# Two-layer hybrid backbone: four modulation parts computed in the first layer's feed-forward

## The chip, the cores and the metric

The kernel runs on one core of a Trainium2 chip. The metric is the device time of one execution in microseconds (us). The kernel before was run three times: median 2722.55 us, lowest 2719.62, highest 2728.21. One more execution was recorded by the hardware profiler, and all rows below are from that one.

## The reference

The reference computes two layers of a diffusion backbone on 512 latent tokens (and 256 context tokens) of width 1024. Every sub-layer begins with a modulated norm, whose shift and scale come from a small vector `c` by way of a large matrix `w_ada`. Cut to what matters here:

```python
def modnorm(x, gain, shift, scale):
    return rms(x) * gain * (1.0 + scale) + shift
...
# per layer: six modulation vectors of width 1024 for the latent tokens
# and six for the context tokens, from one product with w_ada
...
h = modnorm(x, gain1, shift1, scale1)   # norm1: token mixers
# RWKV-7 recurrence, latent attention, Fourier mixing, merged by gates
x = x + gate1 * mixers(h)
h = modnorm(x, gain2, shift2, scale2)   # norm2: gated ConvFFN
x = x + gate2 * ffn(h)
```

The modulation of a layer depends on `c` and `c_ctx` alone, so any of it can be computed at any time before its first use. The kernel cuts the 2 x 6 x 1024 values into 24 parts, named (layer, j, half): j is 0 for the shift and 1 for the scale of norm1, 2 its gate, 3 to 5 the same of norm2, and a half is 512 columns.

## The kernel before

The residual stream lies transposed, channels on partitions, 768 tokens (512 latent, 256 context) along the free axis. All large products keep fp32 accuracy by splitting: a weight tile of 128 columns is loaded raw into a buffer `wr` (512 KB, `load_w`, L186), ACT copies it rounded into `wh` (L183), DVE makes the rest `wl` (L184), and PE runs three passes (high by high, low by high, high by low; L220 for dense products). The raw buffers are a ring of three (`WR_BUFS`) in one pool, shared by all weight loads; `wh` and `wl` have two buffers each. All weight loads are issued by SP's queue, in the order in which the scheduler put them. The scheduler of the framework orders each engine's instructions when the program is built.

A layer goes through these stages: projections of the recurrence (`rwkv_project`), the recurrence in twelve steps (`rwkv_scan`, lines 942 to 1214), the other mixers (`rwkv_out`, `fourier`, `mla`), the merge with its output products, and the ConvFFN with 22 columns f, of which each takes two loads of `w_up` (products `mm` from `fH`, `fL`), a three-tap convolution (`conv`, ACT L229 and DVE L231, L232), a gate (ACT L1400, DVE L1401) and a split into `gH` and `gL`. In layer 0 the gates of the three branches are computed as background work for PE: `gate_part` makes one gate column in 24 products of 512 tokens and 24 of 256 (L688), from two loads split like any weight, and ACT copies the result (`gt`, L693).

`ada_part` (L234) computes one modulation part: four loads of `w_ada`, 512 KB each, into the same ring `wr` (L245); eight matmuls of 32 columns (L258, 16 instructions on PE in the trace), two per load; a copy `row` by ACT (L261); four transposes (L265); and small operations on DVE (L268, L269, for a scale L272). With `ahead` the next load is issued before the current one's products.

The class `Background` (L699) mixes the gate items and the parts between other work. In the recurrence each slot (`after`) allows so many us of background (2.0 in the first 12 slots, then 1.0): gates first, and between their steps a step of a part (`aside`, PSUM tag "a", with `ahead`). After the recurrence `mix` puts the parts that are left between the gate items, and the mixers call `run` with 2.5 us a time (`MFILL`); these parts use the tag "w", which has one buffer and is the gates' too, and load without `ahead`. Parts (0, 0, ·) and (0, 1, ·) are done at the start; `ADA` lists the other 20, and layer 0 takes the first twelve (`ADAS[0]`): ten of them are started in the recurrence, and the last two, (1, 1, 0) and (1, 1, 1), come in the mixers. `ADAF` lists parts for the ConvFFN of layer 0: part f is computed after the code of column f, without `ahead`, with tag "w". It is empty before.

Of the kernel before, what the change touches and what calls it, by code (L numbers as in the profile page):

```python
# [56 lines left out]
WA_BUFS = 12  # L57
NP = (4, 6)
ADA = [(l, j, hf) for l in range(2) for j in range(6) for hf in range(2)][4:]
ADAS = (ADA[:12], ADA[12:])  # L60
ADAF = ()
LEFT = (99, 0)
FRONT = (False, True)
TAGF, TAGO = ("r", "r"), ("s", "r")
# [18 lines left out]
def hybrid_backbone_kernel(ctx: ExitStack, tc: tile.TileContext, A, out, dbg=None):  # L83
# [1199 lines left out]
    for l in range(DEPTH):  # L1283
# [8 lines left out]
        with ExitStack():  # L1292
            gp = far(yst, l, f"gt{l}")

            items = [("m", i) for i in (5, 6, 7, 2, 3, 4, 0, 1)] + [("g", x, c) for c in range(8) for x in range(3)]
            bg = Background(l, items, ADAS[l], hH, hL, streams, gp)
            with ExitStack() as e2:
# [91 lines left out]
        with ExitStack() as es:  # L1389
            fp = near(es, l, f"ff{l}", 2)  # L1390
            for gi, (f0, f1) in enumerate(FGROUPS):
                gH, gL = [], []
                for f in range(f0, f1):
# [12 lines left out]
                    gL.append(lo)  # L1406
                    if l == 0 and f < len(ADAF):
                        for _ in ada_part(*ADAF[f], "w"):
                            pass
# [124 lines left out]
```

## Time and profile before

| | |
|---|---|
| median of three runs | 2722.55 us |
| the profiled execution, its own time | 2723.43 us |
| its span, first to last instruction | 2721.6 us |
| PE (TensorE matmul) busy | 2581.3 us, 95% |
| DVE busy | 1467.6 us, 54% |
| ACT busy | 1075.3 us, 40% |
| mean granted clock | 0.98 |

The stages of layer 0 in the profile, from its start: recurrence about 229 to 579 us, mixers to 760.7 (first attention product), attention to about 858, merge and output products to 997, ConvFFN to about 1567. Busy time of PE is the sum over instructions as the profiler models their ends; a row of several instructions gives the elapsed time from the first start to the last end.

### The profile page before, as it was taken

The numbers are of one execution on the slowest core, as the hardware profiler recorded it, in microseconds if no ns is written. First come the engines' busy times: TensorE is split into PE (matmuls) and PEld (weight loads), VectorE is DVE, ScalarE is ACT, GpSimd is POOL, SyncE is SP. The second block draws the span as 40 slices with busy tenths as digits, with TensorE's granted clock in tenths as the row PEclk, the third lists the DMA queues.
The fourth block names the chain that finished last, engine by engine and source line by source line (L and its number), as shares of the span: only waits on it lengthen the run. The fifth ranks groups of instructions, "written<-read, shape, count | busy, mean of one in ns | idle before, by whom it ended". The sixth has DMA issues, their size and how long they took to land.

```text
span 2721.6 us, 56800 instructions
## 1 busy us (share of the span) xinstructions
PE 2581.3 (95%) x24016; PEld 2062.2 (76%) x24016; DVE 1467.6 (54%) x2965; ACT 1075.3 (40%) x1914; POOL 234.5 (9%) x316
## 2 busy tenths in 40 slices
PE   6999999997999989999999999999988899899999
PEld 3876777776877878888888877677666678778778
DVE  5443555434556665444444564446554767645546
ACT  4452343433464343222222445444433664423333
POOL 0122122200010000000000001312220010000000
PEclk9998999998999999999999999999999999999999
DMA  6366455365323532222212244764434326332334
GB/s 260 95 163 196 151 156 163 106 209 166 98 99 101 158 93 60 64 62 60 66 54 70 79 155 114 234 201 144 141 111 154 117 83 207 101 93 84 100 96 124
DMA packets 161267, 339.45 MB, mean 125 GB/s; under 512 B 32083, under 2 KB 76757, under 8 KB 161013
## 3 DMA queue, kind: packets, MB, share of 16 engines
q1 hardware_dynamic: 124852, 273.93, 32.4%
q0 software_dynamic: 10944, 36.58, 5.1%
q10 hardware_dynamic: 25216, 25.30, 2.8%
q8 instruction: 190, 3.11, 0.5%
q14 instruction: 65, 0.52, 0.1%
HBM read 273.88 MB, written 61.87 MB: 123 GB/s over the span
## 4 chain that ended last, share of the span: by engine, by line
PE 86%; DVE 5%; DMA 4%; ACT 3%; issue 2%; SPq 0%; ACTq 0%; DVEq 0%; POOL 0%; POOLq 0%
PE mm L220 47%; PE w L688 15%; PE st L957 3%; PE i L957 3%; PE mm L567 2%; PE a L258 2%; PE r L595 2%; PE mm L394 2%; PE s L584 1%; DMA wr<-in_w_ada 1%; PE s L871 1%; PE f L957 1%; PE i L954 1%; DVE wl L184 1%; PE f L954 1%
## 5 line engine op out<-in xcount | busy, mean ns | idle before, releaser
L183 ACT ACTIVATE wh<-wr 128x1024 fp32r<-128x1024 f32 (+4 forms) x334 | 302.0, 906 | 378.5 <-PE mm L220 282.8
L184 DVE TENSOR_TENSOR wl<-wr,wh 128x1024 fp32r<-128x1024 f32 (+3 forms) x332 | 342.6, 1034 | 89.2 <-ACT wh L183 86.8
L220 PE MATMUL mm<-fH,wh 128*128 128x512 f32 (+1 forms) x1072 | 225.0, 358 | 10.5 <-DVE ab L232 7.4
L231 DVE SCALAR_TENSOR_TENSOR ab<-mm,prm,ab 128x511 f32<-128x511 f32 (+1 forms) x132 | 86.8, 657 | 264.2 <-ACT ab L229 264.2
L220 PE MATMUL mm<-fH,wl 128*128 128x512 f32 (+1 forms) x1072 | 220.5, 353 | 0.0
L220 PE MATMUL mm<-fL,wh 128*128 128x512 f32 (+1 forms) x1072 | 219.3, 352 | 0.0
L220 PEld LDWEIGHTS mm<-fH,wh 128*128 128x128 f32 x1072 | 178.7, 192 | 42.1 <-issue 6.4
L220 PEld LDWEIGHTS mm<-fH,wl 128*128 128x128 f32 x1072 | 176.1, 189 | 29.9
L220 PEld LDWEIGHTS mm<-fL,wh 128*128 128x128 f32 x1072 | 175.0, 188 | 29.4
L688 PE MATMUL w<-hH,wh 128*128 128x512 f32 (+1 forms) x760 | 183.9, 377 | 10.2 <-ACT gt L693 9.7
L220 PE MATMUL mm<-gH,wh 128*128 128x512 f32 (+1 forms) x568 | 174.5, 346 | 10.0 <-ACT wh L183 4.8
L688 PE MATMUL w<-hL,wh 128*128 128x512 f32 (+1 forms) x760 | 180.5, 366 | 0.0
L688 PE MATMUL w<-hH,wl 128*128 128x512 f32 (+1 forms) x760 | 177.1, 366 | 0.0
L220 PE MATMUL mm<-gH,wl 128*128 128x512 f32 (+1 forms) x568 | 175.4, 348 | 1.1 <-DVE wl L184 0.9
L1252 DVE SCALAR_TENSOR_TENSOR x<-mm,mod,x 128x256 f32<-128x256 f32 (+1 forms) x136 | 80.0, 606 | 175.1 <-PE mm L220 174.4
L220 PE MATMUL mm<-gL,wh 128*128 128x512 f32 (+1 forms) x568 | 171.6, 343 | 0.0
L688 PEld LDWEIGHTS w<-hH,wh 128*128 128x128 f32 x760 | 125.3, 192 | 45.2 <-ACT gt L693 15.7
L229 ACT ACTIVATE ab<-mm,prm 128x768 f32<-128x768 f32 (+1 forms) x88 | 70.0, 795 | 219.9 <-PE mm L220 219.9
L688 PEld LDWEIGHTS w<-hH,wl 128*128 128x128 f32 x760 | 127.1, 191 | 23.5 <-issue 2.5
L688 PEld LDWEIGHTS w<-hL,wh 128*128 128x128 f32 x760 | 124.5, 189 | 24.0 <-issue 4.0
L220 PEld LDWEIGHTS mm<-gH,wh 128*128 128x128 f32 x568 | 97.3, 188 | 29.8 <-ACT wh L183 10.4
L220 PEld LDWEIGHTS mm<-gH,wl 128*128 128x128 f32 x568 | 97.3, 188 | 17.5 <-DVE wl L184 3.7
(388 smaller groups left out, 4631.4 us busy)
## 6 DMA issues: line engine op xcount, KB each, us to landing
wr<-in_w_up SPq DMA_DIRECT2D x88, 512.0 KB, 3.5
wr<-in_w_ada SPq DMA_DIRECT2D x80, 512.0 KB, 5.2
wr<-in_w_g SPq DMA_DIRECT2D x48, 512.0 KB, 4.1
wr<-in_w_out SPq DMA_DIRECT2D x32, 512.0 KB, 3.6
wr<-in_w_dn SPq DMA_DIRECT2D x48, 320.0 KB, 3.0
X<-rwx SPq DMA_DIRECT2D x48, 288.0 KB, 4.7
wr<-in_w_rw SPq DMA_DIRECT2D x24, 512.0 KB, 4.2
wr<-in_w_dn SPq DMA_DIRECT2D x32, 384.0 KB, 3.2
```

What stands on the lines that cost most here:

```text
L183: S.activation(out=H, in_=raw, func=AF.Copy)
L184: e.tensor_tensor(out=L, in0=raw, in1=H.bitcast(F32), op=ALU.subtract)
L220: TE.matmul(ps[:, a:b], lhsT=W[:, k, :], rhs=X[k][:, a:b], start=(k == 0 and n == 0), stop=(k == kt - 1 and n == 2))
L229: S.activation(out=o[:, a:b], in_=ps[:, a:b], func=AF.Identity, scale=w[1])
L231: V.scalar_tensor_tensor(out=o[:, a + 1:b], in0=ps[:, a:b - 1], scalar=w[0], in1=o[:, a + 1:b], op0=ALU.mult, op1=ALU.add)
L258: TE.matmul(ps[32 * i:32 * i + 32], lhsT=cs32[:, k, :], rhs=w[:, k - k0], start=(k < 4), stop=(k >= 4))
L394: TE.matmul(ps[:, o:o + hi - lo], lhsT=X(k)[:, t * 128:(t + 1) * 128], rhs=W[:, k, lo:hi], start=(k == 0 and n == 0), stop=(k == kt - 1 an ...
L567: TE.matmul(ps[:, a:b], lhsT=qT[:, h, t * 128:(t + 1) * 128], rhs=kT[:, h, a:b], start=True, stop=True)
L595: TE.matmul(po[64 * p:64 * p + 64, 0:128], lhsT=Vn[:, j, h * 64:(h + 1) * 64], rhs=pts[p][:, j * 128:(j + 1) * 128], start=(j == kts[0]), ...
L688: TE.matmul(ps, lhsT=w[:, k, :], rhs=X[k][:, a:b], start=(k == 0 and n == 0), stop=(k == 7 and n == 2))
L957: self.i = f(*a, **k)
L1252: V.scalar_tensor_tensor(out=x[:, a:b], in0=ps[:, a:b], scalar=mod[l][:, j, c, s:s + 1], in1=x[:, a:b], op0=ALU.mult, op1=ALU.add)
```

## The change

Eight parts stay beside the recurrence and the mixers of layer 0, and the four parts of layer 1's norm1, shift and scale, two halves each, are listed for the ConvFFN. The loop there is in the kernel before too.

```diff
-ADAS = (ADA[:12], ADA[12:])
-ADAF = ()
+ADAS = (ADA[:8], ADA[12:])
+ADAF = ADA[8:12]
```

The list sets what the scheduler gets, and so the order on the engines. In the mixers, PE's rows around the end of part (1, 1, 1) in the kernel before are these; L1233, L801 and L813 are the head norms of `rwkv_out`, L657 to L660 the Fourier products, and `w_8100` is the part's PSUM tile.

```order
L813 MATMUL s_7678<-cst_75,rex_7676 128x128 x4
L813 MATMUL s_7683<-cst_75,rex_7676 128x128 x2
L258 MATMUL w_8100<-wr_8101,cs32_102 32x512 x2
L1233 MATMUL s_7718<-y_7709,cst_75 128x512
L657 MATMUL r_7955<-dft_7795,z_7818 128x129
L658 MATMUL r_7955<-alt_7798,zh_7819 128x129
L660 MATMUL r_7955<-dft_7795,z_7818 128x127
L1233 MATMUL s_7721<-y_7709,cst_75 128x256
L258 MATMUL w_8100<-wr_8105,cs32_102 32x512 x2
L258 MATMUL w_8100<-wr_8127,cs32_102 32x512 x2
L801 MATMUL s_7725<-cst_75,y1_7710 128x2 x6
L258 MATMUL w_8100<-wr_8131,cs32_102 32x512 x2
```

After the change the same steps of `rwkv_out` (its `s` tiles have other numbers) stand among gate products.

```order
L813 MATMUL s_7626<-cst_75,rex_7624 128x128 x4
L813 MATMUL s_7631<-cst_75,rex_7624 128x128 x2
L688 MATMUL w_8186<-hL2_151,wh_7880 128x256
L688 MATMUL w_8186<-hL3_152,wh_7880 128x256
L688 MATMUL w_8186<-hL4_153,wh_7880 128x256
L688 MATMUL w_8186<-hL5_154,wh_7880 128x256
L688 MATMUL w_8186<-hL6_155,wh_7880 128x256
L688 MATMUL w_8186<-hL7_156,wh_7880 128x256
L657 MATMUL r_7906<-dft_7743,z_7766 128x129
L658 MATMUL r_7906<-alt_7746,zh_7767 128x129
L660 MATMUL r_7906<-dft_7743,z_7766 128x127
L1233 MATMUL s_7666<-y_7657,cst_75 128x512
```

The products L258 are gone from the place, and L688 follow each other there (16 of 512 tokens behind the last row shown, before the next L1233).

At the end of the mixers PE transposes the query heads (L452, one group of six for each of six token tiles), and the attention's first product is L567. Before, gates stand between them; these rows are followed by 22 wide gate products and the last group:

```order
L688 MATMUL w_8974<-hL5_154,wh_8778 128x256
L688 MATMUL w_8974<-hL6_155,wh_8778 128x256
L452 MATMUL mm_8908<-cst_75,qn_8563 96x128 x6
L688 MATMUL w_8974<-hL7_156,wh_8778 128x256
L452 MATMUL mm_8943<-cst_75,qn_8563 96x128 x6
L452 MATMUL mm_8966<-cst_75,qn_8563 96x128 x6
```

Of the kernel after the change, from the last gate products to the attention's first:

```order
L688 MATMUL w_8932<-hL6_155,wh_8784 128x256
L688 MATMUL w_8932<-hL7_156,wh_8784 128x256
L452 MATMUL mm_8771<-cst_75,qn_8503 96x128 x6
L452 MATMUL mm_8808<-cst_75,qn_8503 96x128 x6
L452 MATMUL mm_8834<-cst_75,qn_8503 96x128 x6
L452 MATMUL mm_8872<-cst_75,qn_8503 96x128 x6
L452 MATMUL mm_8899<-cst_75,qn_8503 96x128 x6
L452 MATMUL mm_8921<-cst_75,qn_8503 96x128 x6
L567 MATMUL mm_8985<-kT_7928,qT_7927 128x512
L567 MATMUL mm_8985<-kT_7928,qT_7927 128x256
```

No gate product is left behind the first L452; before, 24 half-wide and 22 wide ones stand between the second group of transposes and the last, and 2 wide and 24 half-wide ones within the attention.

In the ConvFFN, PE's rows at the border of columns 2 and 3, before:

```order
L220 MATMUL mm_11690<-fL6_10725,wh_11684 128x512
L220 MATMUL mm_11690<-fL6_10725,wh_11684 128x256
L220 MATMUL mm_11690<-fL7_10726,wh_11684 128x512
L220 MATMUL mm_11690<-fL7_10726,wh_11684 128x256
L220 MATMUL mm_11817<-fH0_10711,wh_11806 128x512
L220 MATMUL mm_11817<-fH0_10711,wh_11806 128x256
```

and after, with part (1, 1, 0) in `w_11751`:

```order
L220 MATMUL mm_11636<-fL6_10619,wh_11630 128x256
L220 MATMUL mm_11636<-fL7_10620,wh_11630 128x512
L220 MATMUL mm_11636<-fL7_10620,wh_11630 128x256
L258 MATMUL w_11751<-wr_11752,cs32_102 32x512 x2
L258 MATMUL w_11751<-wr_11756,cs32_102 32x512 x2
L258 MATMUL w_11751<-wr_11760,cs32_102 32x512 x2
L258 MATMUL w_11751<-wr_11764,cs32_102 32x512 x2
L265 MATMUL w_11770<-cst_75,row_11768 128x128 x4
L220 MATMUL mm_11790<-fH0_10605,wh_11779 128x512
```

The part's eight products and four transposes stand between the last product of column 2 and the first of column 3. The same is so for part (1, 1, 1) at the border of columns 3 and 4; of part (1, 0, 1) seven eighths at the border of columns 0 and 1, and of part (1, 0, 0) the first load's products stand ahead of column 0 and the others before its context half (rows 4267 to 4271). SP's queue has these loads in this order, with the semaphores each waits for:

```order
L245 DMA wr_11752<-in_w_ada 128x1024 [waits DMAHW6_49,DVE_49]
L245 DMA wr_11756<-in_w_ada 128x1024 [waits DMAHW5_49,PE_49]
L245 DMA wr_11760<-in_w_ada 128x1024 [waits DMAHW7_49,DVE_49]
L245 DMA wr_11764<-in_w_ada 128x1024 [waits DMAHW0_49,PE_49]
L191 DMA wr_11778<-in_w_up 128x1024 [waits DMAHW1_49,PE_49]
L191 DMA wr_11784<-in_w_up 128x1024 [waits DMAHW2_49,PE_49]
L245 DMA wr_11907<-in_w_ada 128x1024 [waits DMAHW3_49,PE_49]
```

Before, the loads of `w_up` follow each other and each waits for DVE (`wl` of the load three places back). Now a load waits for DVE where that buffer held a `w_up` tile and for PE where it held a part's: `wr_11764`, the fourth of part (1, 1, 0), for the products of its first, `wr_11778` and `wr_11784` (column 3) for those of its second and third.

## Rows read from the trace of the kernel before

**Rows 1.** The page, part 4: the chain that ended last, by line.

```profile
PE mm L220 47%; PE w L688 15%; PE st L957 3%; PE i L957 3%; PE mm L567 2%; PE a L258 2%; PE r L595 2%; PE mm L394 2%; PE s L584 1%; DMA wr<-in_w_ada 1%; PE s L871 1%; PE f L957 1%; PE i L954 1%; DVE wl L184 1%; PE f L954 1%
```

**Rows 2.** Windows: us from and to, length, busy of each engine (count), PEclk, DMA share, GB/s.

```profile
579.00:760.70 181.70, 161.34 (x933) 135.69 (x934) 84.86 (x225) 70.55 (x117) 2.30 (x5) 0.92 0.47 154
...
630.00:640.00 10.00, 4.57 (x16) 2.82 (x16) 1.88 (x13) 0.00 (x0) 0.00 (x0) 0.50 0.92 305
...
1022.00:1567.00 545.00, 539.33 (x3033) 467.00 (x3034) 258.63 (x374) 156.13 (x189) 0.00 (x0) 0.99 0.22 66
```

**Rows 3.** Waits of PE, 579 to 761: total us, times, longest.

```profile
PE w L258 <- DMA wr<-in_w_ada: 10.7, 4, 5.4
PE w L688 <- ACT gt L693: 3.9, 3, 2.8
```

**Rows 4.** Timeline of PE, mixers: start, us, instruction, count, idle before and its releaser.

```profile
610.98 1.40 PE L801 MATMUL s<-cst,y 128*128 128x2 f32 x12
...
626.75 1.05 PE L258 MATMUL w<-wr,cs 128*32 128x512 f32 x4 [1.56 <-DMA wr<-in_w_ada]
...
635.09 2.72 PE L801 MATMUL s<-cst,y 128*128 128x2 f32 x12
641.35 1.92 PE L258 MATMUL w<-wr,cs 128*32 128x512 f32 x4 [3.54 <-DMA wr<-in_w_ada]
...
646.01 3.36 PE L688 MATMUL w<-hH,wh 128*128 128x512 f32 x8
...
732.92 2.02 PE L688 MATMUL w<-hH,wh 128*128 128x512 f32 x8
```

**Rows 5.** Products L258 in the recurrence: its group (229 to 580), then one timeline row.

```profile
L258 PE MATMUL a<-wr,cs 128*32 128x512 f32 x148 | 34.4, 604 | 0.1
...
559.37 1.91 PE L258 MATMUL a<-wr,cs 128*32 128x512 f32 x12
```

**Rows 6.** Lines of PE, 579 to 760.7: count, busy us, mean ns, idle before.

```profile
L258 PE MATMUL w<-wr,cs 128*32 128x512 f32 x32 | 9.3, 718 | 10.7 <-DMA wr<-in_w_ada 10.7
...
L265 PE MATMUL w<-cst,row 128*128 128x128 f32 x8 | 1.7, 354 | 0.7 <-ACT row L261 0.7
```

**Rows 7.** Timeline of ACT and of DVE at the query heads.

```profile
733.12 0.74 ACT L505 ACTIVATE jq<-mm,yc 128x576 f32<-128x576 f32 x1
...
749.31 1.69 ACT L453 ACTIVATE qT<-mm,gT 96x768 f32<-96x768 f32 x2
...
744.92 0.62 DVE L446 TENSOR_TENSOR qn<-qn,sw 128x192 f32<-128x192 f32 x2
```

**Rows 8.** Issues of w_up on SP, then landing times of all loads of line 245.

```profile
993.86 4.50 SPq L191 DMA_DIRECT2D wr<-in_w_up  x2
...
DMA to landing us min/median/max: 3.9/5.3/10.2
```

**Rows 9.** Timeline of PE, columns 0 and 1 of the first feed-forward.

```profile
997.03 2.11 PE L220 MATMUL mm<-fH,wh 128*128 128x512 f32 x8 [0.98 <-DVE x L1252]
...
1010.58 3.19 PE L220 MATMUL mm<-fH,wh 128*128 128x256 f32 x15 [1.05 <-ACT fH L332]
...
1016.00 1.72 PE L220 MATMUL mm<-fL,wh 128*128 128x256 f32 x13
1022.82 5.24 PE L220 MATMUL mm<-fH,wh 128*128 128x512 f32 x16 [5.11 <-DVE ab L232]
...
1027.90 2.97 PE L220 MATMUL mm<-fH,wl 128*128 128x512 f32 x16
```

**Rows 10.** Timeline of ACT: a part's row (mixers), wh and gH (columns 0, 1).

```profile
643.32 0.60 ACT L261 ACTIVATE row<-w 128x512 f32<-128x512 f32 x1 [13.59 <-PE w L258]
...
1020.16 1.05 ACT L183 ACTIVATE wh<-wr 128x1024 fp32r<-128x1024 f32 x1
...
1026.47 0.84 ACT L183 ACTIVATE gH<-ab 128x768 fp32r<-128x768 f32 x1 [1.58 <-DVE ab L1401]
```


## The prediction

> **What bounds the kernel now.** I read the chain of waits first, by line: nearly all of it is products on PE, and of the other entries one is a transfer, 1% of the span, for the modulation weights [rows 1]. So PE sets the time, and a change counts by the PE work and the PE idle time that it moves. Next the stages by windows [rows 2]: the feed-forward of layer 0 has PE busy 539.3 of 545 us at a DMA share of 0.22; the mixers, from the last recurrence step to the first attention product, have it busy 161.3 of 181.7 at 0.47. In the mixers' worst stretch, 630 to 640, PE is busy 4.6 of 10 us, the DMA share is 0.92 and the granted clock 0.50, the lower of its two levels (1.2 against 2.4 GHz). The table of waits tells who ends PE's idle time there: the weight loads of `ada_part` (10.7 us in 4 waits), then ACT's copies of gate results (3.9) [rows 3]. The timeline shows the price: a wait of 3.5 us before one load's products, which then take 1.92 us instead of 1.05, and the next work slow too: the head sums at L801 take 2.72 us against 1.40, eight gate products 3.36 against 2.02 [rows 4]. The reader should see that parts 10 and 11 in the mixers are served late, and that the feed-forward has free DMA time but hardly any free PE time.
>
> **Recurrence: two parts leave.** `a` products took 34.4 us for 148, so 16 of them (one part) 3.7 us of busy time; elapsed, 12 took 1.91, so 2.5 a part [rows 5]. Four transposes cost 0.85 (1.7 us for 8) [rows 6]. The slots are filled all the same: by the order, 19 more 512-wide gate products go ahead of the last state, at 0.25 us each (2.02 for 8, [rows 4]) 4.8 us. The gain is 2 x (2.5 + 0.85) - 4.8 = 1.9, or 4.3 with 3.7 a part. I take 2.5, nearer the elapsed figure. The parts' loads leave SP's queue too; the rows give them no wait worth a term.
>
> **Mixers: two parts leave.** From 161.3 us of PE work go 9.3 and 1.7 [rows 6], the slow clock's excess of 1.3 and 1.3 (above), and the gates' difference: 17 wide products fewer (4.2), 24 half-wide more (3.2), for the gates that stood in the attention are now ahead of it. That leaves 146.7. Of 20.4 us idle the 10.7 go, 9.7 stay. New idle comes at the query heads. Now PE covers them with gates: from the last query product (ACT's read of it at 733.12) to the first rotated tile (744.92 and 0.3) are 12 us [rows 7], and PE was busy. After the change the gates have run out: behind the last query product stand nine half-wide gate products (1.2 us) and then all transposes of the heads. The DVE chain is shorter by 0.7 for a narrower weight split, so PE idles 11.4 - 1.2 = 10.2 us, and 1 more because the six groups of transposes follow ACT's copies at 0.85 each (1.69 for two). The stretch is 146.7 + 9.7 + 11.2 = 167.6, 14.1 less than now, and the attention is rid of 2 wide and 24 half-wide products, 3.6. I take a gain of **18**, with scan **20.5**. Bounds: 33 if other work covers the heads; 10 if the waits of `rwkv_out`'s chain, now hidden behind late loads, come to light.
>
> **Feed-forward: four parts arrive.** Their sixteen loads go through the same three buffers as the weights of the columns. In SP's order each column's two loads stand behind the four loads of the part before, and a buffer is free when PE has used it, so a load is issued late and PE then waits for its landing. Nothing in this stage shows such a landing; the `in_w_ada` loads took 3.9 us at least, 5.3 in the median [rows 8]. I take 3.9, as the stage's DMA share is low [rows 2], and keep 5.3 for the range. By the Trainium skill, DMA: Bandwidth & Descriptors, section Anatomy of one DMA, a transfer takes about 2.0 us and its bytes at 436 GB/s; an estimate from it is 3.2 us for 512 KB, and with that the sum would be about 3.5 us lower, over five landings. No row of a 512 KB load of these weights is so short, so the sum stays with 3.9.
> - Part 0 (behind column 0 in the program): its first products stand ahead of column 0's on PE. Column 0 began at 997.03 [rows 9]; the load takes the third place, issued at 993.86 [rows 8], lands at 997.8, and its products take 1.05 [rows 4]: 1.8 us late. Three more loads' products, at 0.64 (a third of 1.91), stand before the context half: 1.9. The transposes (0.85) fit into the 1.05 us that PE waits for `fH` there [rows 9]. Sum 3.7.
> - Part 1: column 0 ended at t0 = 1017.7 and column 1 began 5.1 us later [rows 9]. Now loads 1 and 2 are each issued after the products of the load before: t0 + 3.9 + 1.05 + 3.9 + 1.05 = t0 + 9.9, 4.8 later. Loads 0 and 3 (0.64 each) and the transposes add 2.1. Sum 6.9.
> - Parts 2 and 3: today column follows column without a gap. Now load 3 is issued after load 0's products, and ACT, in order, must copy the row before it makes `gH` and the next column's `wh`, which the column's products need: 0.64 + 3.9 + 1.05 + 0.60 (row) + 0.84 (gH) + 1.05 (wh) = 8.1 us [rows 10], then a start at the low clock, as at 1022.82 after 5.1 us of idling, where sixteen products took 5.24 against 2.97 [rows 9]: 2.3. Sum 10.4 each.
>
> The losses are 3.7 + 6.9 + 20.8 = **31.4** (27 without the clock's fall, 38 at landings of 5.3). DVE's and ACT's small operations of a part hide beside PE as before, other than those named. Net -20.5 + 31.4 = +10.9 on the profiled execution's 2723.4, which lies 0.9 above the median of 2722.55. **Forecast: 2733.5 us**, slower; its own range is 2724 to 2746.
>
> **Rivals.**
> - Hidden loads, not slower: the stage with a DMA share of 0.22 takes sixteen loads without PE seeing them; paid is PE work alone, 4 x (2.5 + 0.85) = 13.4. Then -20.5 + 13.4 gives 2716 (2706 at the gain's upper bound). It decides at the third buffer: if a load is issued a landing (3.9 us) before PE comes to it. Low DMA share speaks for it, the order of buffer releases against: load 3 waits for load 0's products right ahead of it. This is also what the Trainium skill, Perfetto Trace Analysis, section Optimization Strategy, would have one expect: stages with different most-contended engines gain when interleaved. The rows agree that the engines differ [rows 2].
> - Cancelling: the heads' wait is covered, so the gain is about 31 and the losses equal it: 2723. For it: gates may slide less than I read. Against it: the order shows no gate row left there.
> - The mixers give little: with the late loads gone, `rwkv_out`'s own chain (transfers, DVE, PE by turns) ends the waits, the gain is about 8: 2723.4 - 8 + 31.4 = 2747. For it: the chain's steps lie among the late loads [rows 4]; against: PE has gates to fill with until the heads.
>
> **How the numbers follow.** Forecast 0.51, hidden loads 0.15, cancelling 0.20, little gain 0.14. The range 2712 to 2750 leaves out the lower part of the first rival and the ends of the last. A measurement of this kernel can tell about 0.3% (8.2 us) from no change, so bounds are 2714.4 and 2730.7. Faster: about half of the hidden loads and a little of the rest, 0.11. Slower: two thirds of the forecast's case and nearly all of the last, 0.48. Same: 0.41.
>
> **What would show it.** After the change PE's waits for `in_w_ada` are gone between the recurrence and the attention, and appear in layer 0's feed-forward: one around 8 to 11 us in all ahead of each of columns 3 and 4, two landings in a row ahead of column 1. PE idles some 10 us before the heads' transposes. If the columns follow without gaps, the hidden loads are right and I am wrong; if the stretch to the attention stays near 180 us, the last rival is.

## The result, and the profile after

The changed kernel took 2742.05 us (median of 5 runs, 2740.06 to 2750.11) against 2720.45 (2718.54 to 2728.21) of the kernel before on the same chip: ratio 1.0078, 95% interval [1.0054, 1.0103]. The forecast was 2733.5, slower; the measured time lies within the range, and the loss is about double the one forecast. The profiled execution has a span of 2738.3 us, 16.7 more than before.

Both sides of the prediction stand in the new profile. First the waits of PE (total us, times, longest), from the end of the recurrence to the attention:

```profile
PE mm L452 <- DVE qn L446: 10.1, 1, 10.1
PE w L688 <- ACT gt L693: 8.9, 4, 4.1
```

and from 970 to 1200 us, the end of the output products and the first half of the feed-forward's columns:

```profile
PE w L258 <- DMA wr<-in_w_ada: 16.3, 5, 4.2
PE mm L220 <- DVE wl L184: 3.7, 3, 2.3
PE w L265 <- ACT row L261: 2.1, 3, 0.7
```

The loads' waits [rows 3] are gone from the mixers and have come to the feed-forward, 16.3 us where 10.7 were, ahead of columns 0, 1, 3 and 4. The wait at the query heads, 10.1 us, is new, and the waits for ACT's gate copies have grown from 3.9 to 8.9. The stretch from the recurrence to the attention, by windows (from and to, length, busy of PE, PEld, DVE, ACT, POOL, granted clock, DMA share, GB/s; answers to the first of [rows 2]), and the 5 us around the start of column 3:

```profile
571.00:743.50 172.50, 151.17 (x898) 132.87 (x897) 84.76 (x218) 70.69 (x119) 6.55 (x13) 0.93 0.47 160
```

```profile
1060.00:1065.00 5.00, 3.87 (x13) 3.09 (x14) 3.25 (x6) 3.13 (x4) 0.00 (x0) 0.50 0.42 129
```

The border of columns 2 and 3, as the chain that ended last sees it (start, us, what):

```profile
1053.36 1.02 PE w L258 x8
1054.38 4.32 DMA wr<-in_w_ada
1058.70 0.04 issue
1058.74 1.15 PE w L258 x4
1059.89 0.02 issue
1059.91 0.60 ACT row L261
1060.51 0.73 ACT gH L183
1061.25 0.95 ACT wh L183
1062.20 0.04 issue
1062.24 3.99 PE mm L220 x11
```

Three loads' products follow column 2 at once (1.91 us from 1053.29). The fourth load is issued at 1054.38, when the first load's products have freed its buffer, and lands 4.32 us later, and then products, ACT's row, `gH` and `wh` follow one another until column 3 can begin at 1062.24, 8.9 us late and at a clock of 0.50. At the border of columns 0 and 1 two landings follow each other, as forecast:

```profile
1005.17 3.99 DMA wr<-in_w_ada
...
1009.20 1.95 PE w L258 x4
...
1011.16 4.14 DMA wr<-in_w_ada
...
1015.35 1.92 PE w L258 x4
```

PE's timeline has the rest: the heads, part 0's last three loads and transposes, and column 3, which answers to column 1 in [rows 9].

```profile
736.20 7.17 PE L452 MATMUL mm<-cst,qn 128*96 128x128 f32 x36 [10.10 <-DVE qn L446]
743.54 1.99 PE L567 MATMUL mm<-kT,qT 96*128 96x512 f32 x5 [0.16 <-ACT qT L453]
```

```profile
992.95 1.91 PE L258 MATMUL w<-wr,cs 128*32 128x512 f32 x12
...
996.19 0.66 PE L265 MATMUL w<-cst,row 128*128 128x128 f32 x4 [0.69 <-ACT row L261]
...
1062.24 6.00 PE L220 MATMUL mm<-fH,wh 128*128 128x512 f32 x22 [0.56 <-ACT wh L183]
1068.08 2.96 PE L220 MATMUL mm<-fH,wl 128*128 128x512 f32 x16
```

The 36 transposes of the heads took 7.17 us after the idle time, and the first 22 products of column 3 took 6.00, where 16 take 2.96 a little later.

### The profile page after: what moved, and what is told of

The parts are those of the page before. It is cut to its first block, busy times and chain, and to the rows that moved or that the text cites. A ratio compares the mean times of both kernels' runs of the same rounds, so it can differ in the third digit from the quotient of the medians.

```text
span 2738.3 us, 56818 instructions
## 1 busy us (share of the span) xinstructions
PE 2585.5 (94%) x24016; PEld 2059.2 (75%) x24016; DVE 1469.3 (54%) x2965; ACT 1074.9 (39%) x1914; POOL 233.4 (9%) x316
## 4 chain that ended last, share of the span: by engine, by line
PE 86%; DVE 5%; DMA 4%; ACT 3%; issue 2%; SPq 0%; ACTq 0%; DVEq 0%; POOL 0%; POOLq 0%
PE mm L220 47%; PE w L688 15%; PE i L957 3%; PE mm L567 3%; PE st L957 3%; PE a L258 2%; PE r L595 2%; PE mm L394 2%; PE s L584 1%; DMA wr<-in_w_ada 1%; PE s L871 1%; DVE wl L184 1%; PE f L957 1%; PE i L954 1%; DMA raw<-m_dram 1%
## 5 line engine op out<-in xcount | busy, mean ns | idle before, releaser
L220 PE MATMUL mm<-fH,wh 128*128 128x512 f32 (+1 forms) x1072 | 226.4, 360 | 3.9 <-DVE ab L232 1.7
L220 PE MATMUL mm<-fH,wl 128*128 128x512 f32 (+1 forms) x1072 | 219.9, 352 | 0.0
L220 PE MATMUL mm<-fL,wh 128*128 128x512 f32 (+1 forms) x1072 | 219.9, 352 | 0.0
L220 PEld LDWEIGHTS mm<-fH,wh 128*128 128x128 f32 x1072 | 179.7, 193 | 39.2 <-issue 2.5
L220 PEld LDWEIGHTS mm<-fL,wh 128*128 128x128 f32 x1072 | 175.2, 188 | 31.2 <-issue 1.7
L220 PEld LDWEIGHTS mm<-fH,wl 128*128 128x128 f32 x1072 | 175.3, 188 | 29.5
L688 PE MATMUL w<-hH,wh 128*128 128x512 f32 (+1 forms) x760 | 184.2, 378 | 13.2 <-ACT gt L693 13.0
L220 PE MATMUL mm<-gH,wh 128*128 128x512 f32 (+1 forms) x568 | 175.3, 348 | 10.0 <-ACT wh L183 4.4
L688 PE MATMUL w<-hL,wh 128*128 128x512 f32 (+1 forms) x760 | 182.6, 368 | 0.0
L688 PE MATMUL w<-hH,wl 128*128 128x512 f32 (+1 forms) x760 | 178.6, 367 | 0.2 <-issue 0.2
L220 PE MATMUL mm<-gH,wl 128*128 128x512 f32 (+1 forms) x568 | 175.7, 348 | 1.2 <-DVE wl L184 1.0
L220 PE MATMUL mm<-gL,wh 128*128 128x512 f32 (+1 forms) x568 | 172.4, 345 | 0.0
L688 PEld LDWEIGHTS w<-hH,wh 128*128 128x128 f32 x760 | 124.9, 192 | 47.6 <-ACT gt L693 19.4
L688 PEld LDWEIGHTS w<-hH,wl 128*128 128x128 f32 x760 | 127.8, 193 | 23.2 <-issue 2.2
L688 PEld LDWEIGHTS w<-hL,wh 128*128 128x128 f32 x760 | 125.2, 190 | 23.0 <-issue 3.0
L220 PEld LDWEIGHTS mm<-gH,wh 128*128 128x128 f32 x568 | 97.8, 189 | 29.7 <-ACT wh L183 10.4
L220 PEld LDWEIGHTS mm<-gH,wl 128*128 128x128 f32 x568 | 98.0, 189 | 17.9 <-DVE wl L184 4.1
```

The source lines that it names most:

```text
L220: TE.matmul(ps[:, a:b], lhsT=W[:, k, :], rhs=X[k][:, a:b], start=(k == 0 and n == 0), stop=(k == kt - 1 and n == 2))
L688: TE.matmul(ps, lhsT=w[:, k, :], rhs=X[k][:, a:b], start=(k == 0 and n == 0), stop=(k == 7 and n == 2))
```

## Experiments

Each kernel was compared with the kernel before on the same chip (medians of 2725.5 to 2727 there). The table gives the ratio with its interval, and from the profile of each the start of four products, in us from the start of its execution: the recurrence's last (L957), the attention's first (L567), the attention's last output (L595), the last of the feed-forward of layer 0 (L220 on `gH`). The last column is the way from the third to the fourth, that is, what the feed-forward and the merge before it took.

| kernel | ratio | recurrence | attention | its end | feed-forward | between |
|---|---|---|---|---|---|---|
| before | 1 | 578.7 | 760.7 | 856.0 | 1573.4 | 717.4 |
| changed | 1.0078 [1.0054, 1.0103] | 570.8 | 743.5 | 836.9 | 1591.5 | 754.6 |
| e1_own | 0.9993 [0.9977, 1.0009] | 573.5 | 747.2 | 840.5 | 1567.0 | 726.5 |
| e2_two | 0.9983 [0.9970, 0.9997] | 576.6 | 741.6 | 834.9 | 1564.6 | 729.7 |
| e3_spread | 1.0035 [1.0021, 1.0048] | 572.3 | 744.3 | 837.7 | 1579.9 | 742.2 |
| e4_none | 0.9940 [0.9922, 0.9957] | 574.7 | 749.0 | 842.3 | 1562.8 | 720.5 |
| e5_two_own | 0.9946 [0.9928, 0.9964] | 574.4 | 740.5 | 833.9 | 1552.9 | 719.0 |
| e6_two_gap | 0.9965 [0.9947, 0.9984] | 577.0 | 742.2 | 835.5 | 1557.3 | 721.8 |
| e7_mix_ahead | 0.9994 [0.9977, 1.0011] | 575.7 | 758.8 | 854.1 | 1571.9 | 717.8 |
| e8_hold | 0.9925 [0.9897, 0.9952] | 560.5 | 728.5 | 821.9 | 1549.1 | 727.2 |
| e9_ring_hold | 1.0014 [1.0003, 1.0026] | 559.2 | 726.2 | 819.5 | 1575.0 | 755.5 |
| e10_before_hold | 0.9961 [0.9948, 0.9974] | 561.0 | 742.4 | 846.0 | 1562.8 | 716.8 |
| e11_hold3 | 0.9980 [0.9965, 0.9995] | 571.0 | 748.0 | 841.4 | 1569.2 | 727.8 |
| e12_two_hold | 0.9888 [0.9866, 0.9911] | 560.4 | 730.9 | 826.2 | 1546.2 | 720.0 |

Single executions scatter: the changed kernel, e1_own, e3_spread and e4_none have one and the same order on PE up to the output products, and their attention ends between 836.9 and 842.3. Differences of 5 us between two profiles tell nothing. In layer 1, behind the table, the scatter is larger: from its last product to the end the profiles take 1145.8 to 1159.6 us (1148.2 before, 1157.0 in e5_two_own, 1159.6 in e8_hold). So the ratio tells what a kernel is worth, and the table only where time goes.

**e1_own: buffers of their own.**

```diff
-                        for _ in ada_part(*ADAF[f], "w"):
+                        for _ in ada_part(*ADAF[f], "w", wf, bufs=4):
```

(`wf` is a pool on the feed-forward's side that is closed behind column 3; its tiles are `wa` in place of `wr`.)

> The four parts stay behind columns 0 to 3, but their loads have four buffers of their own and no longer share the ring of three with the feed-forward's weights. Theory (late loads: a ring buffer is free only when PE has used it, so PE waits for landings and restarts at the low clock): the 36 us that the feed-forward gave back fall to the products and transposes, four times 2.6 to 3.4 = 10 to 14, so 2711 to 2716 us, and the waits for in_w_ada (16.3 us) are gone. Rival (the work itself costs it: products, transposes, ACT's copy of the row ahead of gH and wh): still 2735 or more.

The ratio falls from 1.0078 to 0.9993, some 23 us, and the way from the attention's end to the feed-forward's from 754.6 to 726.5. PE waits for no load of a part any more; these are its longest waits from 965 to 1570:

```profile
PE mm L220 <- DVE ab L232: 4.7, 2, 3.3
PE mm L220 <- DVE wl L184: 4.1, 5, 2.3
```

So the loss was the shared ring, not the work: 9 us remain against 37. (With their own buffers the scheduler also put most of part 0's products into the wait for column 0's convolution, so the 9 us are not four whole parts. A longer ring, still shared, was not tried.) On the time itself the theory had 4.5 to 9.5 us below the kernel before (2720.5 when it was written); 2724.31 against 2725.54 is 1.2, as the other side gave less than 19 (e4_none): the theory held in the waits and missed in the time. The rival, 15 above, is out.

**e4_none: the gain by itself.**

```diff
-ADAF = ADA[8:12]
+ADAF = ()
+    P.memset(mod[1][:, 0:2], 0.0)
+    P.memset(gsc[1][:, 0], 1.0)
```

> The four parts are left out altogether (layer 1's first norm uses constants in place of its shift and scale), so this shows the gain of taking them from the recurrence and the mixers by itself. Theory: 19 us, as the attention's end moved, so 2700 to 2703. Rival (the attention's end is an illusion and part of it is given back further on in the layer, so the feed-forward costs less than 36): 2706 or more.

The kernel leaves the four parts out, and layer 1's first norm uses constants. 2710.53 against 2725.54: 15 us, with an interval of 12 to 21. The rival's bound was 14.5 us (2706 against 2720.5), the theory's 17.5 to 20.5, so the interval takes in both, and the middle stands at the rival's edge. In its profile the attention ends 13.7 us earlier than before. So taking the four parts away is worth about 15 us, and with the changed kernel's 21.6 (interval 15 to 28) the feed-forward's cost comes to 36.6, near the table's last column (37.2).

**e2_two: the mixers' parts alone.**

```diff
-ADAS = (ADA[:8], ADA[12:])
-ADAF = ADA[8:12]
+ADAS = (ADA[:10], ADA[12:])
+ADAF = ADA[10:12]
```

> Only the mixers' two parts move (behind columns 0 and 1); the recurrence keeps its ten. Theory: the mixers' gain comes whole (11 to 14 us to the attention's end), the feed-forward gives back 6.1 + 5.2 for the parts at columns 0 and 1: 2717 to 2721, no difference that can be told. Rival (the gain comes mostly from the recurrence, whose end moved by 7.9 us in the changed kernel): gain 5 at most, 2726 or more.

2722.07 against 2725.54, 3.5 us less: the theory's bounds were 3.5 below to 0.5 above the kernel before, the rival's 5.5 above or more, so the rival is out. Two parts moved bring the attention's end forward by 21.1 us, where 11 to 14 were expected, and no less than four. The waits from 570 to 760 tell why:

```profile
PE w L688 <- ACT gt L693: 5.8, 5, 3.4
...
PE mm L452 <- ACT qT L453: 0.8, 2, 0.6
```

No wait of 10.1 us at the heads: with the recurrence's parts in place 19 wide gate products fewer are done in it, and 24 half-wide ones still stand between the heads' transposes. So, as far as single profiles tell, moving the recurrence's two parts took nothing off the path to the attention's end; what the recurrence lost (its end, 570.8 against 576.6) came back as the wait at the heads.

**e3_spread: one load per column.**

```diff
-                    if l == 0 and f < len(ADAF):
-                        for _ in ada_part(*ADAF[f], "w"):
-                            pass
+                    if l == 0:
+                        ada_step(f)
```

(`ada_step` takes the part's generator one load further, and at the fifth column does row, transposes and sums.)

> The same four parts, the same ring, but one load with its two products per column instead of four loads at one column (row, transposes and sums at the fifth): each load has a whole column to land. Theory (late loads): no wait is left, the feed-forward pays the work alone, 10 to 14 us, so 2711 to 2716. Rival (sharing the ring by itself, or the work, costs): 2730 or more.

The waits went, as the theory had it (1.9 us are left), but the time is 2735.73 against 2725.54, 1.0035, at the rival's bound of 9.5 us above. Of the rival's two reasons it was the work. The lines of PE show it, in e1_own and then here (count, busy us, mean ns, idle before):

```profile
L258 PE MATMUL w<-wa,cs 128*32 128x512 f32 x64 | 9.6, 628 | 0.0
```

```profile
L258 PE MATMUL w<-wr,cs 128*32 128x512 f32 x64 | 16.8, 605 | 1.9 <-DMA wr<-in_w_ada 1.9
```

The same 64 instructions took 9.6 us mostly in groups of 16 and 16.8 in groups of four, though each lasts as long (628 and 605 ns). On the timelines a group of four between two columns takes 1.05 us, one of sixteen 1.92:

```profile
1066.91 1.05 PE L258 MATMUL w<-wr,cs 128*32 128x512 f32 x4
```

```profile
1018.91 1.92 PE L258 MATMUL w<-wa,cs 128*32 128x512 f32 x16
```

In the traces, four of the sixteen start within 0.03 us, and the next four about 0.45 us after them; in a group of four, two start and then two. So one load's products alone leave half of what can run side by side unused, and twelve take as long as sixteen (1.91, part 0 above).

Column follows column at 18.0 us here and at 16.8 without a part; a whole part at one border costs 2.5 (19.3 in e1_own). Sixteen groups at 1.2, the transposes of four parts and 1.9 of waits make 24 of the 25 us of the table. So the shared ring costs little if each load has time, but small groups of these products are dear. Small groups with buffers of their own were not tried.

**e5_two_own and e6_two_gap: two parts, own buffers.** e5_two_own is e1_own with the lists of e2_two; e6_two_gap puts both parts behind column 0:

```diff
+                    if l == 0 and f == 0:
+                        for a in ADAF:
+                            for _ in ada_part(*a, "s", wf, bufs=8):
+                                pass
```

> Only the mixers' two parts move (behind columns 0 and 1), and their loads have four buffers of their own. Theory (late loads, and gates that still cover the query heads since the recurrence keeps its parts): the mixers' gain of e2_two stays (21 us to the attention's end by its trace), the feed-forward gives back about 5 (2.5 a part) in place of 12: 7 us below e2_two, 0.994 of the kernel before, and no wait of PE for the loads in either place. Rival (the four parts' order was the matter and the ring is not): as e2_two, 0.998.

> As e5_two_own, but both parts behind column 0, with eight buffers, so that their products stand in the 5.1 us for which PE waits for the convolution there anyway. Theory: nearly nothing is given back (0 to 3 us), 0.992 to 0.994 of the kernel before. Rival (the products delay the next column's start by their own length, since its conv is what is late and the work of ACT and DVE for the parts comes on top): 0.995 or more.

e5_two_own came out as expected: 0.9946, and 719.0 us on the way where the kernel without the parts had 720.5. Part 0's products lie in the wait for column 0's convolution, which shrinks to 2.57 us from 5.11, and column 1 starts at the full pace, with 3.08 us for 16 products and not 5.24 [rows 9]; part 1 costs 2.5.

```profile
1001.45 3.08 PE L220 MATMUL mm<-fH,wh 128*128 128x512 f32 x16 [2.57 <-DVE ab L232]
```

e6_two_gap, 0.9965, does not gain on it. Its second part did not fall into the gap but in four groups into column 1's products, at 1.05 us each, and between the first part's groups PE waited for landings (0.74 and less). Its rival expected 0.995 or more, but for another reason, the lateness of the convolution, and the profile does not show that.

**e7_mix_ahead: ask earlier, move nothing.**

```diff
-                return ada_part(it[1], it[2], it[3], "w")
+                return ada_part(it[1], it[2], it[3], "w", ahead=True)
```

> The kernel before with nothing moved; the two parts in the mixers ask for each load one step ahead. Theory (loads late because the ring's buffers are freed late and the DMA queues are full there): the program's order of issue changes little, so half of the 10.7 us of waits goes at most; 0.998 to 1.000. Rival (the loads are late only because the code asks for them late): the waits go, 11 to 17 us, 0.994 to 0.996.

0.9994, no change, and the wait is what it was [rows 3]:

```profile
PE w L258 <- DMA wr<-in_w_ada: 10.6, 4, 5.0
```

But the edit did not make the loads earlier: SP's queue issues its 789 transfers in the same order in both kernels. So the run decides nothing between the theory and the rival. It shows only that the place of the request in the code does not set the issue here. SP's own waits in the kernel before, from 580 to 640 us, say what held these loads:

```profile
SPq L245 <- PE w L258: 7.4, 4, 3.8
SPq L245 <- DMA wr<-in_w_ada: 3.9, 2, 2.1
```

The larger share is a wait for a part's own products to free a buffer. How much the full queues add was not told apart.

**e8_hold to e12_two_hold: gates held back.** All have 7 or 3 in place of 12 slots of 2.0 us:

```diff
-FIRST = ((12, 2.0), (8, 3.0))
+FIRST = ((7, 2.0), (8, 3.0))
```

e8_hold is e1_own with it, e9_ring_hold the changed kernel, e10_before_hold the kernel before, e12_two_hold is e5_two_own; e11_hold3 is e1_own with 3.

> As e1_own (four parts moved, own buffers), but 7 in place of 12 slots of the recurrence allow 2.0 us of background, so that gates are held back for the mixers. Theory (with the recurrence's two parts gone, gates are used up early and nothing covers the query heads, 10 us): PE's wait of 10.1 us at the heads shrinks to 2 at most, the gates' work leaves the recurrence, so 4 to 8 us below e1_own, about 0.997 of the kernel before. Rival (the wait there is hidden or is taken up by the attention): as e1_own, 0.999.

> The changed kernel (shared ring, four loads at a column) with the gates held back as in e8_hold (7 slots of 2.0 us in place of 12). Theory (two separate losses: the ring in the feed-forward, and the uncovered query heads): the feed-forward still gives back some 36 us, the heads' wait of 10.1 us is gone, so it lies as far below the changed kernel (1.0078) as e8_hold below e1_own (0.007): 1.000 to 1.002. Rival (e8_hold's gain needs the parts' own buffers, since the ring is what the held gates' loads wait for): 1.005 or more.

> The kernel before with the same 7 slots and nothing moved. Theory: its query heads are covered and its gates only go from the recurrence to the attention, so it stays as it is: 0.998 to 1.001. Rival (a shorter background in the first slots is a gain by itself, whatever is moved): 0.995 or less.

> As e8_hold, with 3 slots of 2.0 us. Theory: the heads are covered already at 7 (wait 1.1 us), so holding more gates back gives nothing more: 0.991 to 0.994, as e8_hold. Rival (the gain of e8_hold is the recurrence's shorter slots, which go on paying): 0.990 or less.

> As e5_two_own (the mixers' two parts alone, own buffers), with 7 slots of 2.0 us. Theory: there the gates cover the heads without it, so nothing is gained on e5_two_own: 0.993 to 0.996. Rival (the shorter slots are a gain by themselves): 0.990 or less.

In e8_hold the wait at the heads is nearly gone:

```profile
721.39 1.10 PE L688 MATMUL w<-hL,wh 128*128 128x256 f32 x8
722.33 1.47 PE L452 MATMUL mm<-cst,qn 128*96 128x128 f32 x12
724.87 1.49 PE L452 MATMUL mm<-cst,qn 128*96 128x128 f32 x12 [1.07 <-DVE qn L446]
```

The last gate products now end as the first tiles are ready. But e8_hold gained 0.0068 on e1_own, some 18 us where 4 to 8 were expected, and e10_before_hold and e12_two_hold gained where the theory gave them nothing: 0.0039 and 0.0058. So holding back is a gain by itself, as the rivals had it (e12_two_hold reached its rival's bound of 0.990, e10_before_hold at 0.9961 neither 0.998 nor 0.995), and the theory was too narrow. The attention's end seems to separate the two effects: where the heads were covered before, it moved by 10.0 (before to e10) and 7.7 (e5 to e12); where they were not, by 18.6 (e1 to e8) and 17.4 (changed to e9). The difference, 7 to 11 us, is about the 9 by which the wait at the heads shrank. The runs' own times do not show that split: they gained 10 and 16 us where the heads were covered and 18 and 17 where not, each uncertain by 4 to 9 us, so its size rests on single profiles. The first effect lies in the recurrence. Its end came 17.7 us earlier in e10_before_hold, for 24 wide and 24 half-wide gate products fewer (9.1 us at 0.25 and 0.13); part of the rest is less idling of PE in it. From 300 to 400, of the kernel before, of e10_before_hold and of e11_hold3:

```profile
300.00:400.00 100.00, 95.77 (x2184) 74.39 (x2182) 54.99 (x137) 39.52 (x103) 21.73 (x28) 1.00 0.46 141
```

```profile
300.00:400.00 100.00, 98.66 (x2247) 74.69 (x2235) 57.49 (x144) 39.86 (x106) 25.18 (x32) 1.00 0.51 149
```

```profile
300.00:400.00 100.00, 95.37 (x2089) 70.94 (x2086) 51.34 (x129) 39.23 (x100) 24.64 (x31) 1.00 0.53 160
```

PE is busy 98.7 of 100 us with 7 slots, and 95.8 and 95.4 with 12 and 3 (e11_hold3 is built on e1_own, where it is 96.2 with 12 and 99.6 with 7). At 3, moreover, PE waits 15.2 us for gate copies in the mixers, and e11_hold3, 0.9980, met neither expectation. So of the three numbers tried 7 is best; that it is a matter of where the gates fall between the recurrence's steps is likely, but the cause stays open. e9_ring_hold met its expectation, 1.0014: the feed-forward still took 755.5.

**The version that beats both** is e12_two_hold, 2695.75 us against 2726.97, 0.9888 [0.9866, 0.9911]: the mixers' two parts in the feed-forward with buffers of their own, the recurrence's parts where they were, and fewer gates in the first slots.

## Why the prediction was right, and where it was off

- The sign held, and so did the mechanism of the loss: late loads in the feed-forward. Rival "hidden loads" failed at the third buffer, where the prediction said it would be decided; with own buffers (e1_own) its case becomes true, and what is left is the work.
- By the Trainium skill (Perfetto Trace Analysis, Optimization Strategy) performance may be improved by interleaving stages with different most-contended engines. The rows do not show that these two stages differ so, as the prediction read them: PE is the busiest engine in both (161.3 of 181.7 us and 539.3 of 545 [rows 2]), and the DMA share of 0.92 belongs to 10 us. The runs fall on both sides: the change 1.0078, e5_two_own 0.9946. What decided was the moved loads' buffers.
- Borders of columns 2 and 3, and 3 and 4: forecast 8.1 and 2.3 for the clock, 10.4 each; measured 8.9 and 2.1, 11.0, at the first (column ends at 1053.3 and 1081.1, 27.8 apart, where 16.8 is the pace), and 9.4 and 1.5 at the second. The landing was 4.32, not 3.9.
- Parts 0 and 1: forecast 3.7 + 6.9 = 10.6, measured 13.7 (column 2's end lies 5.4 us ahead of the kernel before, the attention's end 19.1). The two serial landings took 3.99 and 4.14, and the products behind them 1.92 each, at a granted clock of 0.50, where the prediction had 1.05: that is 1.7 of the 3. Part 0's other products ahead of the context half took 1.91, as forecast, and PE waited 0.69 for its row besides.
- The landing: the estimate from the Trainium skill (DMA: Bandwidth & Descriptors, Anatomy of one DMA) was 3.2 us, the row's lower bound 3.9; the chain shows 3.99, 4.14 and 4.32. The row decides, and it was itself a little low. (The page gives its fit for transfers issued by GpSimd; these are issued by SP.)
- Sum of the feed-forward: 31.4 forecast, 37.2 by profile, 36.6 by the runs (1.5 us of it at a later column, in other kernels too).
- The heads: idle time 10.2 forecast, 10.1 measured. Behind it PE was busy 7.17 us with the 36 transposes, where the kernel before has 4.74; the prediction had allowed 1 us for ACT's pace.
- The gain: 20.5 forecast to the attention's end; 13.7 to 19.1 in the four profiles of the same order, 15 by e4_none's time, with an interval of 12 to 21 that takes in the forecast. Between recurrence and attention PE was to be busy 146.7 and idle 20.9 of 167.6 us; it is busy 151.2 and idle 21.3 of 172.5. So the idle time came out in sum, but not in its parts: the waits for gate copies grew from 3.9 us to 8.9, and the other waits that were to stay (for `Vn` 2.5, and shorter ones) shrank. With the parts gone, gates follow gates through the one buffer of tag "w", and PE waits for ACT's copy more often; that this is the reason is read from the order and was not tried.
- **The step that failed** is the price of the low clock behind the new waits. The prediction priced it in one place, 2.3 us at each of columns 3 and 4. "That leaves 146.7" takes the old waits' slow work out of the mixers and puts none in for the new waits, and the products behind the two landings in a row are counted at 1.05 us. The changed kernel shows the clock at its lower level, 0.50, in these places too (windows as above):

```profile
578.30:585.10 6.80, 5.82 (x25) 5.62 (x26) 0.96 (x1) 0.90 (x3) 0.00 (x0) 0.50 1.01 377
736.20:742.10 5.90, 5.90 (x28) 5.28 (x29) 1.87 (x9) 3.22 (x4) 0.00 (x0) 0.50 0.00 1
1009.20:1011.20 2.00, 1.92 (x4) 0.19 (x4) 2.00 (x4) 0.46 (x2) 0.00 (x0) 0.50 0.00 0
```

The first is behind a wait for a gate copy. There eight half-wide gate products take 2.07 us, where eight took 1.22 just before:

```profile
570.95 1.22 PE L688 MATMUL w<-hH,wh 128*128 128x256 f32 x8
...
579.28 2.07 PE L688 MATMUL w<-hH,wh 128*128 128x256 f32 x8 [4.06 <-ACT gt L693]
```

The second is the heads' transposes, the third the products at the border of columns 0 and 1. In the mixers the clock stands at 0.50 for 23.8 us, with PE busy in 15.0 of them; before, with the late loads, it was 27.3 and 17.9. So the low clock moved with the waits instead of leaving. The transposes' excess is 2.4 us, and that of the half-wide gates at 0.50, 39 against 15 before, by estimate as much (at 0.13 us each at full speed). Together that is about the 4.5 us by which PE was busy longer in the mixers than forecast; smaller terms of either sign stand beside it. In the feed-forward it is 1.7 of the 5.8 us of extra cost (37.2 for 31.4); longer landings, the wait for the row and the later column make most of the others. In this profile the recurrence's end, 5.4 us earlier than forecast, happened to make up for the mixers' 4.9, so that its gain (19.1) looks nearer to the forecast than its terms were. By the runs, 5.5 us of the 10.7 between the loss and its forecast (21.6 and 10.9) lie on the side of the gain (15 for 20.5) and 5.2 in the feed-forward, within intervals about as wide as these terms.
- Two readings were off. The prediction took twelve of the part's products in 1.91 us as 0.64 a load and 2.5 a part; sixteen take 1.92 (e5_two_own), as they run four at a time. And the 2706 of the rival "hidden loads" does not follow from its terms: a gain of 33 with losses of 13.4 gives 2703 or less.
- The recurrence: 2.5 forecast, 4 to 8 in the four profiles, but given back at the heads, as e2_two shows; moving those two parts was worth nothing that can be told.
- "Cancelling" failed, as the heads' wait was not covered; "the mixers give little" failed too, since `rwkv_out`'s chain did not come to light.

## What to carry to other kernels

Before moving work that loads data into a quieter stage, see which buffer each load waits for, and who frees it: a stage with free DMA time hides nothing if the load's buffer is freed by the products right ahead of it. Moved work is also cover that is taken away; look for the next chain that it hid. Where a wait goes, its slow clock goes with it, and where a new wait comes, price the work behind it at the lower clock. And keep products of this kind together.

## What was unexpected

Four of the 32-column products (L258) between dense ones take 1.05 us and sixteen 1.92, so the same 64 took 16.8 us spread and 9.6 together. And the number of slots in which the recurrence takes gates makes 10 us by itself (0.9961 with 7 in place of 12), and most of such a gain is lost again with 3 (on e1_own: 0.9993 with 12, 0.9925 with 7, 0.9980 with 3).
